# Two blocks of a small model: two linear-attention heads' values and the queries are projected between the second and third forgetting-attention pair, the fourth pair last but for the gates

## The chip, the cores and the metric

The kernel runs on one core of one Trainium2 chip. The metric is the device time of one launch in microseconds. The kernel before was timed three times: median 2360.22 us, lowest 2359.61, highest 2360.74.

## The reference, cut to what matters

A sequence of 528 rows (16 learned rows and 512 of the input, 1024 wide) passes through two layers of a first block and one layer of a second one. The change touches only the mixer of the first block, which each of its two layers runs once:

```python
xn = rms_norm(h, attn_norm[i])
gq, gk, gv, gr, glr, fq, fk, fv, ff = jnp.split(xn @ w_in[i], cuts, axis=-1)
# gated linear attention, 4 heads: per chunk of 64 rows a state S = decay*S + k^T v; out = q @ S
o_gla = rms_norm(gla_chunk_causal(gq/8, gk, gv, log_a), gla_norm) * silu(gr)
# forgetting attention, 8 heads of 64: softmax(q k^T / 8 + c_t - c_s) v, causal
o_fox = rms_norm(forgetting_attention(fq, fk, fv, log_f), fox_norm)
h = h + concatenate([o_gla, o_fox]) @ w_out[i]
```

## The kernel before, in words

**Jobs.** The work is a list of projection jobs. A job multiplies 128 columns of a weight by the whole sequence, 528 rows as two halves of 264. Float32 accuracy is had by splitting weight and activation into a rounded high part and a rest, so each of the 8 k-steps has three passes of two matmuls and a job has 48 matmuls (`steps`, line 304, matmul on line 322). A job accumulates into one of two PSUM buffers (`psm`, line 49). When its matmuls are done, its evacuation copies the result out, scaled by the row's norm (`scaled`, line 374: VectorE on line 378 or 380); the buffer is then free for the job after the next. Weights come by DMA on SP's queue, 256 columns (two jobs) a load, and are split on ScalarE and VectorE (lines 273 and 274) two jobs ahead.

**Steps behind the jobs.** An evacuation also pushes small functions into a queue: transposes, attention units, norms. While a later job issues its matmuls, `steps` takes functions from the queue at a rate of 1.3 for each k-step and issues their instructions between the matmuls (`pump`, line 299). So functions ride along with later jobs, and what is pushed late rides late.

**The mixer's jobs**, after a small one for the gates of decay. Names: fk, fq, fv with p = 0 to 3 are keys, queries and values of a pair of forgetting-attention heads; gk0 and gk1 are the keys of two linear-attention heads each, gq0 and gq1 the queries; gv0 to gv3 and gr0 to gr3 the values and output gates of one head. The order before is

```
gk0 gk1 fk0 fq0 fv0 | fk1 fq1 fv1 gv0 gv1 | fk2 fq2 fv2 gv2 gv3 | fk3 fq3 fv3 gq0 gq1 | gr0 gr1 gr2 gr3
```

and then the eight jobs of the output projection, `out0` to `out7`, whose k-steps read `mix[0..3]` (linear-attention heads) and `mix[4..7]` (forgetting pairs) in the order 4, 5, 6, 7, 0, 1, 2, 3.

**A forgetting pair** (`fox_pair`, line 630) is ten units, for each of two heads and five row blocks: scores with softmax (Exp on ScalarE, line 575), transposes of the weights (line 600), values (line 620). A unit's stages are pushed one behind the other, so that units overlap in a pipe. Then follow `fox_norm` (line 647: transposes on line 654, VectorE 655, ScalarE 659, VectorE 661 and 186, a power on GpSimd 187), `fox_scale` (line 668) and `fox_tail` (line 672: transposes 681, ScalarE 682, VectorE 182), which writes `mix[4 + p]`. For pairs 0 to 2 these ride in the pipe. For pair 3 the pipe is emptied at once into the queue, `fox_scale` is pushed by gq0's evacuation and `fox_tail` by gq1's.

**Linear attention.** gv3's evacuation pushes the states (line 740, a chain on VectorE), each gq's the outputs and their norms (`gla_out`, lines 794 to 801 and 754). The scaling by the norm (line 762) is pushed by gq1 for heads 0 and 1 and by gr0 for heads 2 and 3. A gr's evacuation applies Silu on ScalarE (line 915). `gla_tail` (line 816: transposes 824 and 828, VectorE 829, ScalarE 830, VectorE 179) makes `mix[h]`; for h = 0 and 1 it is queued, for h = 2 and 3 it is issued inside `out0`, ahead of the k-step of index 2 and 4.

**Order.** Each engine runs its own list strictly in order. The framework makes these lists when the kernel is built, from what is ready by its own costs and from priorities. Evacuations get a raised priority; instructions wrapped in `pin` (lines 668, 681, 762, 824, 828) stay behind the instruction issued before them on their engine. Nothing moves at run time.

Of the kernel before, what the change touches and what calls it, by code (L numbers as in the profile page):

```python
# [36 lines left out]
class Net:  # L37
# [592 lines left out]
    def fox_pair(self, st, i, p, mix, last):  # L630
        self.push(lambda: self.fox_prep(st, p), lambda: self.fox_gates(st, p))
        for b in range(2):
            self.push_unit(self.fox_unit(st, b, 0, None))
        for hf in range(2):
            for b in range(2):
                group = {}
                for j in (2 * hf + 1, 2 * hf + 2):
                    stages = self.fox_unit(st, b, j, group)
                    if hf == 1 and b == 1 and j == 4:
                        stages += [lambda: self.fox_norm(st)]  # L640
                        if not last:
                            stages += [None, lambda: self.fox_scale(st), lambda: self.fox_tail(st, i, p, mix)]
                    self.push_unit(stages)
        if last:
            self.drain_pipe()
# [193 lines left out]
    def layer(self, i):  # L839
        nc, a = self.nc, self.a  # L840
        w_in = a["w_in"][i]
        st = dict(e=[], dec=[], kt=[], gvt=[], S={}, S0={}, om={}, on={}, gr={}, gk={}, gq={}, gv={}, scale={})
        fst = [dict() for _ in range(4)]
        mix = [None] * 8
# [27 lines left out]
        def ev_fk(p):  # L872
            return lambda ps: self.fox_k(fst[p], self.scaled(ps, FULL, self.rs))

        def ev_fq(p):
            def f(ps):
                t = self.scaled(ps, FULL, self.rs, extra=0.125)
                fst[p]["q"] = [self.stack_q(t, b) for b in range(2)]
            return f

        def ev_fv(p):
            def f(ps):
                fst[p]["fv"] = self.scaled(ps, FULL, self.rs)
                self.fox_pair(fst[p], i, p, mix, p == 3)
            return f

        def ev_gk(m):
            def f(ps):
                t = self.scaled(ps, FULL, self.rs)
                self.push(lambda: self.gla_k(st, m, t))  # L890
            return f
# [10 lines left out]
        def ev_gq(m):  # L902
            def f(ps):
                self.gla_q(st, m, self.scaled(ps, FULL, self.rs, extra=0.125))
                self.push(*self.gla_out(st, m))
                if m == 0:
                    self.push(lambda: self.fox_scale(fst[3]))
                else:
                    self.push(*st["scale"][0], lambda: self.fox_tail(fst[3], i, 3, mix))
            return f  # L910

        def ev_gr(h):
            def f(ps):
                t = self.scaled(ps, FULL, self.rs)
                nc.scalar.activation(t, t, AF.Silu)
                tail = lambda: self.gla_tail(st, i, h, t, mix)
                if h == 0:
                    self.push(tail, *st["scale"][1])
                elif h == 1:
                    self.push(tail)  # L920
                else:
                    first_out["at"] = {**first_out.get("at", {}), 2 * h - 2: [tail]}
            return f

        rest = [(256, ev_gk(0)), (384, ev_gk(1))]
        rest += [(512 + 128 * h, ev_gv(h)) for h in range(4)]
        rest += [(0, ev_gq(0)), (128, ev_gq(1))]
        pieces = []
        for p in range(4):
            fox = [(2064 + 128 * p, ev_fk(p)), (1552 + 128 * p, ev_fq(p)), (2576 + 128 * p, ev_fv(p))]  # L930
            r = rest[2 * p:2 * p + 2]
            pieces += r + fox if p == 0 else fox + r
        pieces += [(1024 + 128 * h, ev_gr(h)) for h in range(4)]
        for x in range(0, len(pieces), 2):
            (c0, e0), (c1, e1) = pieces[x:x + 2]
# [11 lines left out]
        def ev_out(k):  # L947
            def f(ps):
                h = self.h[k]
                nc.vector.tensor_tensor(self.v(h, TO), self.psv(ps, TO), self.v(h, TO), op=ALU.add)  # L950
                if k == 0:
                    nxt["hs"] = []
                    nxt["acc"] = self.G()
                    if t0:
                        nc.gpsimd.memset(nxt["acc"][:, :t0], 1.0)
                nxt["hs"].append(self.hs_of(h[:, t0:], self.vec("ffn", 8 * i + k), None, t0, L))
                self.sq_acc(nxt["acc"], h[:, t0:], k == 0, 1.0, t0, L)
            return f
# [4 lines left out]
        for k in range(KT):  # L963
            if k % 2 == 0:
                ch = self.chunk([(self.wcols(w_out, 128 * k, 256), 0)], KT)
            self.job(ch, 128 * (k % 2), lambda: mix, TO, ev_out(k))
            if k == 0:
                first_out = self.jobs[-1]
            self.jobs[-1]["order"] = [4, 5, 6, 7, 0, 1, 2, 3]
            self.jobs[-1]["flush"] = k == 0  # L970


# [699 lines left out]
```

## Time and profile before

| | us |
|---|---|
| median of 3 runs | 2360.22 |
| the profiled execution | 2361.31 |
| its span | 2359.5 |
| TensorE (PE) busy | 2318.5 |
| VectorE (DVE) busy | 1378.4 |
| ScalarE (ACT) busy | 952.2 |
| GpSimd (POOL) busy | 248.3 |

The span is the time from the first to the last instruction; the profiled execution adds 1.8 us around it. The mixer of the first layer lies at about 40 to 262 us of the span, that of the second at about 720 to 942 us. An engine's busy time is an average over stages with different limits. PE's idle time is 41 us in all, and the question for this kernel is where it lies.

### The profile page before, as it was taken

Reading aid. Unit: us, or ns where it says so; the run is one execution under the profiler, and the core shown is the slowest. Engines: PE = TensorE matmul, PEld = TensorE weight load, DVE = VectorE, ACT = ScalarE, POOL = GpSimd, SP = SyncE. Lnnn points to the kernel's source line nnn. Section 1 sums busy time; section 2 is a strip of 40 time slices with the busy share of each in tenths; the row PEclk is TensorE's granted clock in tenths of the full one; section 3 lists DMA queues with packets and bytes.
Section 4 is the critical chain, followed back from the end, with each engine's and each line's share of the span. In section 5 each row is a group of like instructions: output and inputs, shape, how many; then the busy total and the mean of one; then the engine's idle time right before and its main releaser. Section 6 shows DMA issues by size and latency. Waiting matters only on the chain.

```text
span 2359.5 us, 37628 instructions
## 1 busy us (share of the span) xinstructions
PE 2318.5 (98%) x15703; PEld 2133.4 (90%) x15703; DVE 1378.4 (58%) x2480; ACT 952.2 (40%) x1641; POOL 248.3 (11%) x261
## 2 busy tenths in 40 slices
PE   7999999999999999999999999999999999999998
PEld 6999999999998998999998889988999888888888
DVE  6667556465556677466464666797454454333335
ACT  6555434233346655343242544322233533222225
POOL 3111210000021112200000121100000002101012
PEclk9999999999999999999999999999999999999999
DMA  4211122222231211222223222222212222232323
GB/s 115 73 55 55 55 90 90 90 90 89 96 87 54 55 55 54 90 90 90 90 84 105 85 76 88 90 90 90 89 55 72 72 90 90 92 105 89 98 85 130
DMA packets 217072, 196.77 MB, mean 83 GB/s; under 512 B 8987, under 2 KB 214791, under 8 KB 216903
## 3 DMA queue, kind: packets, MB, share of 16 engines
q1 hardware_dynamic: 216903, 194.37, 25.9%
q8 instruction: 124, 2.03, 0.3%
q14 instruction: 45, 0.37, 0.1%
HBM read 192.26 MB, written 2.10 MB: 82 GB/s over the span
## 4 chain that ended last, share of the span: by engine, by line
PE 66%; ACT 1%; DVE 1%; issue 1%; POOL 0%; DMA 0%; POOLq 0%; ACTq 0%; SPq 0%
PE mm L322 59%; PE valuesT L1158 1%; PE scoresS L1141 1%; PE foxV L620 1%; PE attend_pT L480 1%; PE foxT L600 0%; ACT wh L273 0%; PE foxS L510 0%; POOL g L204 0%; PE spreadS L223 0%; PE foxS L511 0%; PE idx L510 0%; DMA raw<-in_w_down_dram 0%; PE to_tokensT L463 0%; PE idx L511 0%
## 5 line engine op out<-in xcount | busy, mean ns | idle before, releaser
L322 PE MATMUL mm<-g,wh 128*128 128x264 f32 (+3 forms) x9168 | 1883.0, 316 | 13.8 <-DVE g L378 11.7
L322 PEld LDWEIGHTS mm<-g,wh 128*128 128x128 f32 x9168 | 1393.3, 190 | 113.8 <-issue 12.8
L322 PE MATMUL mm<-g,wl 128*128 128x264 f32 (+3 forms) x4552 | 1161.0, 313 | 0.0
L322 PEld LDWEIGHTS mm<-g,wl 128*128 128x128 f32 x4552 | 752.2, 189 | 50.4
L273 ACT ACTIVATE wh<-raw 128x1024 fp32r<-128x1024 f32 (+1 forms) x369 | 384.9, 1043 | 947.9 <-PE mm L322 808.8
L274 DVE TENSOR_TENSOR wl<-raw,wh 128x1024 fp32r<-128x1024 f32 (+1 forms) x369 | 445.1, 1206 | 66.0 <-ACT wh L273 55.8
L378 DVE TENSOR_TENSOR g<-mm,g 128x528 f32<-128x528 f32 (+2 forms) x228 | 158.5, 696 | 318.7 <-PE mm L322 315.4
L204 POOL TENSOR_TENSOR g<-g,g 128x528 f32<-128x528 f32 (+3 forms) x49 | 71.4, 1469 | 914.9 <-ACT g L203 568.0
L179 DVE TENSOR_TENSOR g<-g,g 128x512 fp32r<-128x512 f32 (+3 forms) x131 | 92.1, 703 | 38.2 <-ACT g L1010 29.0
L1035 DVE TENSOR_TENSOR g<-mm,g 128x528 f32<-128x528 f32 (+1 forms) x48 | 33.6, 700 | 119.3 <-PE mm L322 119.3
L992 ACT ACTIVATE g<-g,cv 128x528 f32<-128x528 f32 (+1 forms) x88 | 72.1, 819 | 17.8 <-DVE g L378 17.7
L1421 POOL TENSOR_TENSOR g<-g,g 128x512 f32<-128x512 f32 x22 | 38.9, 1766 | 283.9 <-ACT g L1420 283.9
L995 DVE SCALAR_TENSOR_TENSOR g<-g,cv,g 128x526 f32<-128x526 f32 (+1 forms) x88 | 66.9, 760 | 3.1
L994 DVE SCALAR_TENSOR_TENSOR g<-g,cv,g 128x527 f32<-128x527 f32 (+1 forms) x88 | 66.3, 754 | 1.8 <-ACT g L992 1.8
L179 DVE TENSOR_TENSOR g<-foxT,g 128x128 fp32r<-128x128 f32 (+1 forms) x160 | 50.5, 340 | 20.3 <-ACT g L605 18.0
L1006 ACT ACTIVATE g<-g 128x528 f32<-128x528 f32 (+1 forms) x44 | 28.1, 639 | 84.0 <-DVE g L995 84.0
L1008 DVE TENSOR_TENSOR g<-g,g 128x528 f32<-128x528 f32 (+1 forms) x44 | 30.8, 701 | 32.4 <-ACT g L1006 32.4
L575 ACT ACTIVATE g<-g,sm 128x144 f32<-128x144 f32 (+2 forms) x80 | 43.1, 538 | 16.0 <-DVE sm L571 15.3
L187 POOL TENSOR_TENSOR sm<-sm,mhalf 128x10 f32<-128x10 f32 (+3 forms) x29 | 37.2, 1290 | 115.2 <-DVE sm L186 114.9
L605 ACT ACTIVATE g<-foxT 128x256 fp32r<-128x256 f32 (+1 forms) x96 | 33.1, 345 | 27.6 <-PE foxT L600 22.5
L1010 ACT ACTIVATE g<-g 128x528 fp32r<-128x528 f32 (+1 forms) x44 | 28.1, 638 | 33.1 <-DVE g L1008 33.1
L1452 DVE TENSOR_TENSOR g<-mm,g 128x512 f32<-128x512 f32 x16 | 11.1, 692 | 49.9 <-PE mm L322 49.9
(282 smaller groups left out, 1706.8 us busy)
## 6 DMA issues: line engine op xcount, KB each, us to landing
raw<-in_w_up_dram SPq DMA_DIRECT2D x50, 1024.0 KB
raw<-in_w_in_dram SPq DMA_DIRECT2D x44, 1024.0 KB
raw<-in_w_down_dram SPq DMA_DIRECT2D x28, 896.0 KB
raw<-in_w_in_dram SPq DMA_DIRECT2D x28, 512.0 KB
raw<-in_w_out_dram SPq DMA_DIRECT2D x12, 1024.0 KB
raw<-in_w_down_dram SPq DMA_DIRECT2D x12, 1024.0 KB
raw<-in_w_gate_dram SPq DMA_DIRECT2D x10, 1024.0 KB
raw<-in_w_up_dram SPq DMA_DIRECT2D x10, 512.0 KB
```

Source lines behind the costliest of these rows:

```text
L179: (eng or self.nc.vector).tensor_tensor(out, x, hi.bitcast(F32), op=ALU.subtract)
L187: self.nc.gpsimd.tensor_tensor(out, v[:rows, :n], self.mhalf[:rows, :n], op=ALU.pow)
L204: nc.gpsimd.tensor_tensor(acc[:, t0:t1], tmp[:, t0:t1], acc[:, t0:t1], op=ALU.add)
L273: keep(nc.scalar.activation(hi[:, :K], src, AF.Copy))
L274: keep(nc.vector.tensor_tensor(lo[:, :K], src, hi[:, :K].bitcast(F32), op=ALU.subtract))
L322: nc.tensor.matmul(ps[:, b, :n], lhsT=w[:, k, :], rhs=x[:, t:t + n], start=(ki == 0 and pi == 0), stop=(ki == len(order) - 1 and pi == len ...
L378: self.nc.vector.tensor_tensor(self.v(out, toks), self.psv(ps, toks), self.v(rs, toks), op=ALU.mult)
L575: nc.scalar.activation(P[:qs, :N], P[:qs, :N], AF.Exp, scale=-1.0, bias=m, accum_out=col)
L992: nc.scalar.activation(A[:, lo:], U[:, lo:], AF.Identity, bias=self.vec("cb", 44 * i + t), scale=cw(2))
L994: nc.vector.scalar_tensor_tensor(A[:, s1:], U[:, s1 - 1:L - 1], cw(1), A[:, s1:], op0=ALU.mult, op1=ALU.add)
L995: nc.vector.scalar_tensor_tensor(A[:, s0:], U[:, s0 - 2:L - 2], cw(0), A[:, s0:], op0=ALU.mult, op1=ALU.add)
L1421: nc.gpsimd.tensor_tensor(z[:, META:], z[:, META:], self.rs[:, META:], op=ALU.mult)
```

## The change

Only the order of the mixer's jobs and of what rides along with them changes; no instruction of the computation is added or removed. The new order of the jobs is

```
gk0 gk1 fk0 fq0 fv0 | gv0 fk1 fq1 fv1 gv1 | gv2 gv3 gq0 gq1 fk2 fq2 fv2 | fk3 fq3 fv3 | gr0 gr1 gr2 gr3
```

Pair 3's `fox_scale` and `fox_tail` ride in its pipe as those of the other pairs do. All scaling of linear attention is pushed by gq1. The tails of heads 2 and 3 move to index 0 and 2 of `out0`, and all output jobs read `mix` in the order 4, 5, 6, 0, 1, 2, 3, 7. The loads per layer stay five of two adjacent column blocks and seven pairs of loads of one block each.

```diff
@@ fox_pair
                     if hf == 1 and b == 1 and j == 4:
                         stages += [lambda: self.fox_norm(st)]
-                        if not last:
-                            stages += [None, lambda: self.fox_scale(st), lambda: self.fox_tail(st, i, p, mix)]
+                        stages += [None, lambda: self.fox_scale(st), lambda: self.fox_tail(st, i, p, mix)]
                     self.push_unit(stages)
@@ layer, ev_gq
                 self.push(*self.gla_out(st, m))
-                if m == 0:
-                    self.push(lambda: self.fox_scale(fst[3]))
-                else:
-                    self.push(*st["scale"][0], lambda: self.fox_tail(fst[3], i, 3, mix))
+                if m == 1:
+                    self.push(*st["scale"][0], *st["scale"][1])
@@ layer, ev_gr
-                if h == 0:
-                    self.push(tail, *st["scale"][1])
-                elif h == 1:
+                if h < 2:
                     self.push(tail)
                 else:
-                    first_out["at"] = {**first_out.get("at", {}), 2 * h - 2: [tail]}
+                    first_out["at"] = {**first_out.get("at", {}), 2 * h - 4: [tail]}
@@ layer
-            r = rest[2 * p:2 * p + 2]
-            pieces += r + fox if p == 0 else fox + r
+            pieces += {0: rest[:2] + fox, 1: rest[2:3] + fox + rest[3:4], 2: rest[4:] + fox, 3: fox}[p]
@@ layer, output jobs
-            self.jobs[-1]["order"] = [4, 5, 6, 7, 0, 1, 2, 3]
+            self.jobs[-1]["order"] = [4, 5, 6, 0, 1, 2, 3, 7]
```

## Rows read from the trace of the kernel before

**Rows 1.** The page: busy time by engine, and the chain of waits.

```profile
PE 2318.5 (98%) x15703; PEld 2133.4 (90%) x15703; DVE 1378.4 (58%) x2480; ACT 952.2 (40%) x1641; POOL 248.3 (11%) x261
...
PE 66%; ACT 1%; DVE 1%; issue 1%; POOL 0%; DMA 0%; POOLq 0%; ACTq 0%; SPq 0%
```

**Rows 2.** PE's waits, whole span: us in total, times, longest.

```profile
PE mm L322 <- DVE g L378: 11.7, 3, 4.8
```

**Rows 3.** PE's first matmuls of `out0`, both layers: start, us, instruction, idle before.

```profile
258.67 1.22 PE L322 MATMUL mm<-g,wh 128*128 128x264 f32 x4 [3.49 <-DVE g L378]
...
938.99 0.72 PE L322 MATMUL mm<-g,wh 128*128 128x258 f32 x4 [3.49 <-DVE g L378]
```

**Rows 4.** VectorE at the end of the projections, first layer (same columns).

```profile
252.88 1.29 DVE L762 TENSOR_TENSOR g<-g,sm 128x512 f32<-128x512 f32 x2
...
254.42 0.89 DVE L829 SCALAR_TENSOR_TENSOR g<-gla_tailT,cv,g 128x272 f32<-128x272 f32 x2
256.06 1.22 DVE L274 TENSOR_TENSOR wl<-raw,wh 128x1024 fp32r<-128x1024 f32 x1 [0.75 <-ACT wh L273]
257.21 0.70 DVE L179 TENSOR_TENSOR g<-g,g 128x528 fp32r<-128x528 f32 x1
257.82 1.32 DVE L378 TENSOR_TENSOR g<-mm,g 128x528 f32<-128x528 f32 x2
```

**Rows 5.** Windows of 2 us: engines' busy us, granted PE clock, DMA share, GB/s.

```profile
258.00:260.00 2.00, 1.33 (x6) 1.36 (x7) 1.14 (x2) 1.26 (x2) 0.00 (x0) 0.51 0.00 0
260.00:262.00 2.00, 2.00 (x11) 2.00 (x11) 0.00 (x0) 0.00 (x0) 0.00 (x0) 0.50 0.03 8
...
938.00:940.00 2.00, 1.01 (x8) 1.04 (x9) 1.46 (x3) 1.12 (x2) 0.00 (x0) 1.00 0.00 0
```

**Rows 6.** Evacuations of the output jobs: `out0` to `out2` first layer, `out0` second.

```profile
268.72 0.71 DVE L950 TENSOR_TENSOR g<-mm,g 128x528 f32<-128x528 f32 x1 [0.85 <-PE mm L322]
...
274.55 0.71 DVE L950 TENSOR_TENSOR g<-mm,g 128x528 f32<-128x528 f32 x1 [3.01 <-PE mm L322]
...
280.39 0.71 DVE L950 TENSOR_TENSOR g<-mm,g 128x528 f32<-128x528 f32 x1 [3.03 <-PE mm L322]
...
946.48 0.69 DVE L950 TENSOR_TENSOR g<-mm,g 128x516 f32<-128x516 f32 x1 [0.84 <-PE mm L322]
```

**Rows 7.** Pair 3's norm, first layer, from its transposes to `mix[7]`.

```profile
236.68 0.38 PE L654 MATMUL foxN<-ident,g 128*128 128x128 f32 x2
...
242.97 0.83 DVE L668 TENSOR_TENSOR o<-o,sm 128x640 f32<-128x640 f32 x1
...
245.19 0.93 ACT L682 ACTIVATE g<-foxN,cv 128x272 fp32r<-128x272 f32 x2
...
249.13 0.48 DVE L182 SCALAR_TENSOR_TENSOR g<-foxN,cv,g 128x256 fp32r<-128x256 f32 x1
```

**Rows 8.** ScalarE around the first Silu: the last softmax before it, and its table load.

```profile
228.96 0.73 ACT L575 ACTIVATE g<-g,sm 128x528 f32<-128x528 f32 x1
...
237.13 1.28 ACT L915 ACT_TABLE_LOAD   x1
```

**Rows 9.** Windows in the columns of rows 5: three mixer stretches, one of the second block.

```profile
200.00:220.00 20.00, 19.86 (x158) 18.50 (x158) 14.56 (x45) 12.00 (x38) 5.68 (x9) 1.00 0.16 54
220.00:240.00 20.00, 19.49 (x157) 18.28 (x155) 12.81 (x38) 14.08 (x39) 0.90 (x3) 1.00 0.17 53
240.00:260.00 20.00, 16.51 (x131) 16.28 (x132) 17.43 (x35) 10.66 (x21) 7.89 (x8) 0.95 0.16 54
180.00:200.00 20.00, 19.77 (x161) 19.10 (x160) 17.60 (x43) 6.87 (x13) 1.09 (x2) 1.00 0.17 53
...
1835.00:1845.00 10.00, 10.00 (x55) 8.33 (x54) 5.51 (x15) 7.43 (x12) 0.00 (x0) 1.00 0.25 86
```

**Rows 10.** VectorE by line, 180 to 262 us: busy us, mean ns, idle before.

```profile
L740 DVE SCALAR_TENSOR_TENSOR g<-g,dec,gla_statesS 64x128 f32<-64x128 f32 x28 | 9.1, 347 | 0.7
...
L754 DVE TENSOR_REDUCE sm<-g 128x4 f32<-128x512 f32 (+1 forms) x6 | 3.5, 589 | 0.0
```

## The prediction

> **What bounds the kernel now.** I read the page's busy times first. PE is busy for 2318.5 of 2359.5 us, and the chain of waits that ended last is two thirds PE [rows 1]. No edit here changes PE's instructions, so only PE's 41 us of idle time can move, together with the time it spends at half clock. The waits of PE, longest first, come second: the first row puts 11.7 us in three waits down to a projection matmul that waits for line 378 on VectorE, the evacuation of a job [rows 2]. The timeline of PE places two of the three: they stand right ahead of the first matmul of `out0`, 3.49 us in each layer [rows 3]. The third is at the start of the second layer's mixer and is not touched. So the stage that counts is the end of the projections, and the wait that ends last there is a VectorE one.
>
> VectorE's timeline tells what it did instead [rows 4]. `out0` needs the PSUM buffer of gr2. PE had stopped at 258.67 - 3.49 = 255.18 us, at the end of gr3; gr2 had ended one job and two tails earlier, near 248. Its evacuation runs at 257.82, together with gr3's. Ahead of it in VectorE's list stand the scaling of heads 2 and 3 (line 762), the tails of heads 0 and 1 (lines 829, 179) and a weight split (line 274). VectorE is busy 17.43 of the 20 us from 240 to 260, against 14.56 and 12.81 in the two windows before [rows 9]. It is full there because everything that was pushed late rides there.
>
> After the wait the granted clock is 0.51 and 0.50 in the first layer and 1.00 in the second [rows 5]. What this costs comes from `out0` itself: from PE's restart to its evacuation it takes 268.72 - 258.67 = 10.05 us in the first layer and 946.48 - 938.99 = 7.49 us in the second [rows 3, 6]. The second has 258 columns instead of 264, some 0.13 us of a job of 280.39 - 274.55 = 5.84 us [rows 6]. So the half clock costs 2.4 us.
>
> **The change part by part.** I counted through the code which step rides with which job.
>
> *What leaves the end.* Before, the outputs of linear attention and their norms ride in gr1, the scaling (762) and both tails in gr2. Now the outputs ride in gq1 and fk2 and all the scaling in fk2. What gr1 to gr3 lose on VectorE is six reduces of line 754, 3.5 us [rows 10], and the scaling of four heads, 2 x 1.29 us [rows 4], some 6 us, and the GpSimd powers ahead of them.
>
> *What comes to the end.* Pair 3's units rode in gq0, gq1 and gr0 and ride now in gr0, gr1 and gr2. Its norm, scale and tail were issued in gr1 and gr2 and are now issued in gr3, steps 0 and 2; the tails of heads 0 and 1 go from gr2 to gr3, steps 3 and 4. The decisive point is that no tail is issued any more before gr2's evacuation. In gr2 there are only units, as in gr0 before, and the windows that held units have PE at 19.86 and 19.49 of 20 us [rows 9]. So I expect gr2's evacuation inside gr3's time, and the wait of 3.49 us goes in both layers: 2 x 3.49 = 7.0 us. Bounds: 0 (another order of VectorE's list, below) to 7.0. With it goes the half clock, 2.4 us; bounds 0 (another idle time brings it back) to 2.4.
>
> *What is late next.* `mix[7]`. From the transposes of the norm to its last instruction it took 249.61 - 236.68 = 12.9 us [rows 7]. Of this, 7.1 us go to the end of the scale (243.80), and after ScalarE's part ended at 245.19 + 0.93 = 246.12 VectorE came to the last piece only at 249.13, 3 us later, because of the work that now is gone. Without that the chain is 246.12 + 2 x 0.48 - 236.68 = 10.4 us. It can begin 0.8 us into gr3 (after k-step 0) and in the worst case at the end of gr3's own matmuls, 5.8 us, so `mix[7]` is ready 11.2 to 18.7 us after gr3 began. It is needed in the last k-step of `out0`. The two tails in `out0` cost 7.49 - (5.84 - 0.13) = 1.8 us; gr3 has two tails and nine more transposes, so 5.84 + 1.8 + 1.0 = 8.6 us (the 1.0 an estimate: half a tail); the last k-step begins 7 x 0.73 + 1.8 = 6.9 us later, at 15.5 us. PE waits between 0 and 3.2 us here. I take 1.0 us a layer, nearer to the lower end, as the late start is the rarer one: 2.0 us in both.
>
> *Tails of heads 2 and 3.* They are issued two k-steps earlier and `mix[2]`, `mix[3]` are read one earlier, which leaves one k-step (0.73 us) more between. Nothing to pay, provided gr3's evacuation isn't late; if it is, as gr2's was, the bound is again 3.49 us a layer.
>
> *What comes to the middle.* States, outputs and scaling fall in gq0, gq1 and fk2. VectorE then has there 32 x 0.347 = 11.1 us of states [rows 10], 3.5 + 2.6 of norms, three evacuations of 0.7 and three splits of 1.22, together 23 us, against three jobs of 5.84 us and the small matmuls between them. It is a full stretch. The nearest one is 180 to 200 us, with the states in it: VectorE 17.60, PE 19.77 [rows 9]. I take 0; bounds 0 and 3.49 us a layer. What spills over has fq2 behind it, in which nothing rides. PE's order of transposes can shift by tenths of a microsecond either way; that is 0.
>
> *ScalarE's tables.* Before, the last softmax is at 228.96 us and the first Silu brings a table load of 1.28 us at 237.13, one a layer [rows 8]. Now the Silus of gr0, gr1 and gr2 come among pair 3's softmaxes, so up to five loads, four more: 5.1 us of ScalarE a layer. In the windows of the units ScalarE is busy 12.00 and 14.08 of 20; with the loads some 78%. In the second block, where softmaxes and sigmoids alternate, ScalarE is busy 7.43 of 10 us and PE 10.00 of 10 [rows 9]. I cost them at 0; upper bound 5.1 us a layer. The Trainium skill, in "ScalarE: Activation LUTs", section "Table sets: the hidden batching unit", says to do all calls of one table set before those of another, and this change breaks that rule; its section "What ACT_TABLE_LOAD costs" puts a switch at 2.66 us with a drain, of which our row shows 1.28 and no drain. By that figure it would be an estimated 10.6 us of ScalarE a layer.
>
> *Loads.* Their number and sizes stay, and the DMA engines are used at 0.16 to 0.17 in these windows [rows 9]. SP's queue only takes them in another order: 0.
>
> *The sum.* -7.0 - 2.4 + 2.0 = -7.4 us. The profiled execution took 2361.31 us (its span 2359.5 and 1.8 around it), so 2353.9; it lies 1.1 us above the median of the runs shown, so for a median I take 2360.2 - 7.4 = 2352.8, rounded to 2353.
>
> **The rivals.**
>
> *The wait stays.* VectorE's list is made when the kernel is built, and the trace doesn't say why gr2's evacuation was put behind the tails although its priority is raised. If the same order comes again for gr3 or gr2, `out0` or its tails wait as before. For it: the tails of heads 0 and 1 still ride with a gr job, and the same sequence is in both layers. Against it: the four scalings ahead of them are gone. Time: 2360, or about 2356 if one layer gains.
>
> *The wait moves to the middle.* The 23 us of VectorE work make the evacuation of gq0 or gq1 late, and fk2 or fq2 wait for a PSUM buffer: 2 x 3.49 us given back, 2358 to 2360. Against it: 180 to 200 us.
>
> *The last pair ends too late (slower).* This is one chain: table loads stretch pair 3's softmaxes, its units run on into gr3, and its norm begins and ends late, with only one job behind it where three were before. At worst 18.7 + 5.1 = 23.8 us against 15.5: PE waits 8.3 us in `out0`, and with the half clock behind it 10.7 us a layer. That is 21.4 - 9.4 = 12 us slower, 2372. It decides from 9.4 / 2 = 4.7 us a layer on, that is a wait of 2.3 us with the half clock behind it. For it: PE waits in its order and there is no other job to fill in. Against it: PE at 10.00 of 10 where tables alternate [rows 9]. The Trainium skill's rule on table sets would have it so.
>
> **How the numbers follow.** The forecast (2351 to 2355.5, likeliest 2353) gets 0.50; the wait that stays 0.22; the wait in the middle 0.08; the slower case 0.20, most of it between 2362 and 2368. No change that can be told is within 0.2%, or 4.7 us, here 2355.5 to 2364.9. Faster: 0.50 and 0.03 of the one-layer case. Slower: 0.19. The low end is the sum without the 2.0 us, 2350.8, less 1 us for small waits of PE in the windows of the units (20 - 19.49 and 20 - 19.86, in two layers [rows 9]), so 2349.5. The high end reaches into the slower case, 2365.5.
>
> **What would show it.** In the changed kernel, the wait of `out0`'s first matmul for line 378 is gone from both layers; VectorE's list has gr2's evacuation ahead of lines 829; the window behind has clock 1.00; there are three to five table loads among pair 3's softmaxes and no PE wait in their stretch; a wait, if any, stands ahead of `out0`'s last k-step, for line 182, and is under 2.3 us. It is wrong if a wait for line 378 is still there or stands in gq1 to fq2, or if line 182 (or 179) holds PE for over 2.3 us.

## The result and the profile after

The changed kernel takes 2383.99 us (median of 4 runs, 2382.68 to 2385.43), the kernel before 2359.91 in the same comparison. The ratio is 1.0101, 95% interval 1.0090 to 1.0113: 24.1 us slower. I had forecast 7 us faster. The profiled execution has a span of 2382.3 us, 22.8 more than before.

In the changed kernel the line numbers have shifted: `fox_norm` is on lines 646 to 661, `fox_scale` on 667, the tail's transposes on 680, linear attention's tail on 823 to 829, Silu on 912, the evacuation of an output job on 944. Up to line 638 nothing has moved.

From the page, the busy times, which answer to [rows 1]:

```profile
PE 2332.7 (98%) x15703; PEld 2142.3 (90%) x15703; DVE 1379.0 (58%) x2480; ACT 965.0 (41%) x1649; POOL 250.2 (11%) x261
```

PE issues the same 15703 instructions and is busy 14.2 us longer; the same matmuls run slower, in part at half clock (below). ScalarE has eight instructions more, the table loads: 8 x 1.28 = 10.2 of the 12.8 us by which it is busier. VectorE is as busy as before.

PE's waits of the whole span, longest first (us in total, times, longest), against [rows 2]:

```profile
PE foxN L680 <- DVE o L667: 7.3, 2, 3.6
PE mm L322 <- DVE g L378: 4.8, 1, 4.8
PE foxV L620 <- DVE g L179: 4.7, 4, 1.7
```

The wait of `out0` for line 378 is gone from the list in both layers; the one left stands at the start of the second layer's mixer, as before. By this view alone the forecast would look right. In its place stand the tail of pair 3, which waits for its scaling, and pair 3's units, which wait for their weights' low parts (179).

What filled the wait is seen on PE's timeline of the first layer (start, us, instruction, idle before), which answers to [rows 3]:

```profile
247.09 0.41 PE L322 MATMUL mm<-g,wl 128*128 128x264 f32 x2
...
252.84 0.80 PE L620 MATMUL foxV<-g,fvms 128*128 128x256 f32 x2 [1.68 <-DVE g L179]
...
258.02 1.91 PE L620 MATMUL foxV<-g,g 128*128 128x256 f32 x8
...
260.01 1.23 PE L322 MATMUL mm<-g,wh 128*128 128x264 f32 x4
...
263.34 0.41 PE L322 MATMUL mm<-g,wl 128*128 128x264 f32 x2
267.36 1.30 PE L680 MATMUL foxN<-ident,o 128*128 128x128 f32 x5 [3.61 <-DVE o L667]
269.35 0.47 PE L823 MATMUL gla_tailT<-ident,om 128*128 128x128 f32 x1 [0.69 <-DVE g L182]
...
270.84 0.47 PE L823 MATMUL gla_tailT<-ident,om 128*128 128x128 f32 x1 [0.17 <-DVE g L828]
...
271.99 1.55 PE L322 MATMUL mm<-g,wh 128*128 128x264 f32 x4
```

gr3's matmuls end at 247.50; before, they ended at 255.18. PE is 7.7 us early there, because the gates' matmuls have run ahead of pair 3's units. From 247.50 to 260.01 it has only the units, each stage of which waits for another engine: 12.5 us. It is not all idle: from 248 to 260 us PE is busy 8.6 of the 12 us, from 252 on at half clock. Then come 18 matmuls, the three k-steps of `out0` that read `mix[4]` to `mix[6]`. From 263.75 to 271.99 there is no projection again, 8.2 us: the norm, scale and tail of pair 3, then two tails of linear attention. Five k-steps of `out0` are still to come, but the next two read `mix[0]` and `mix[1]`, and the tails that make these (269.35 and 270.84) stand behind pair 3's tail in PE's list. So none of the five runs beside the norm. The second layer has the same two gaps.

VectorE's timeline of the same stretch, for [rows 4]:

```profile
256.64 1.30 DVE L179 TENSOR_TENSOR g<-foxT,g 128x256 fp32r<-128x256 f32 x3 [0.44 <-ACT g L605]
257.86 0.70 DVE L378 TENSOR_TENSOR g<-mm,g 128x528 f32<-128x528 f32 x1
260.44 0.42 DVE L624 TENSOR_TENSOR g<-foxV,g 64x256 f32<-64x256 f32 x1 [1.88 <-ACT g L622]
261.70 0.69 DVE L654 TENSOR_TENSOR o<-foxN,sm 128x512 f32<-128x512 f32 x1 [0.84 <-PE foxN L653]
...
266.38 0.83 DVE L667 TENSOR_TENSOR o<-o,sm 128x640 f32<-128x640 f32 x1 [2.07 <-POOL sm L187]
```

The evacuation of gr2 runs at 257.86. Before, it ran at 257.82. It is as late as it was; only what stands ahead of it is another thing, the units' line 179 instead of the tails. Since PE itself was held by a unit until then, no wait for line 378 shows. The chain of the norm after it, 261.70 to 267.21, is a wait of one engine for the next. The evacuation of `out0`, line 944, comes at 282.09, where it came at 268.72 [rows 6].

Windows of 2 us in the columns of [rows 5]:

```profile
250.00:252.00 2.00, 0.80 (x4) 0.45 (x4) 2.00 (x7) 1.31 (x5) 0.00 (x0) 1.00 0.78 275
252.00:254.00 2.00, 1.17 (x5) 1.17 (x6) 1.18 (x5) 0.49 (x3) 0.00 (x0) 0.53 0.00 0
254.00:256.00 2.00, 2.00 (x11) 1.79 (x9) 0.21 (x1) 0.38 (x1) 0.00 (x0) 0.50 0.00 0
...
264.00:266.00 2.00, 0.00 (x0) 0.00 (x0) 0.28 (x2) 0.00 (x0) 1.81 (x2) 0.95 0.00 0
266.00:268.00 2.00, 0.65 (x3) 0.68 (x4) 0.83 (x1) 0.00 (x0) 0.35 (x1) 0.50 0.00 0
...
274.00:276.00 2.00, 2.00 (x11) 2.00 (x11) 1.81 (x4) 0.61 (x2) 0.00 (x0) 0.50 0.00 0
276.00:278.00 2.00, 2.00 (x18) 2.00 (x18) 1.29 (x3) 0.84 (x2) 0.00 (x0) 0.99 0.00 0
```

The granted clock falls to half (1.2 of 2.4 GHz) at 252 us, inside the first stretch, comes back at 262 and falls again at 266, inside the second: some 20 us at half clock in this layer. For [rows 9], the windows of 20 us (same columns), with the clock at 1.00 in those before them:

```profile
240.00:260.00 20.00, 16.60 (x104) 14.79 (x104) 10.76 (x31) 11.89 (x28) 0.00 (x0) 0.80 0.16 53
260.00:280.00 20.00, 15.54 (x87) 14.09 (x86) 10.68 (x20) 7.17 (x11) 2.16 (x2) 0.68 0.00 1
```

In the kernel before, PE had 131 matmuls from 240 to 260 us; here it has 104, and 87 in the next 20 us, with VectorE at 10.8 and 10.7 us instead of 17.4. No engine is full there.

ScalarE, for [rows 8]: the table loads among pair 3's softmaxes and the last softmax.

```profile
225.75 1.28 ACT L912 ACT_TABLE_LOAD   x1
...
231.08 1.28 ACT L575 ACT_TABLE_LOAD   x1
...
240.30 1.28 ACT L912 ACT_TABLE_LOAD   x1
...
242.43 1.28 ACT L575 ACT_TABLE_LOAD   x1
...
251.23 0.73 ACT L575 ACTIVATE g<-g,sm 128x528 f32<-128x528 f32 x1
...
260.43 1.28 ACT L912 ACT_TABLE_LOAD   x1
```

Five loads, as counted in the prediction. The last softmax comes at 251.23; before, it was at 228.96.

The place of the loss can be fixed by PE's progress: the time from the mixer's first projection matmul to its n-th one, changed kernel less kernel before, worked out from the traces. (That first matmul is at 13.96 and 700.26 us in the kernel before; the 40 and 720 us given above as the mixer's start are too late.) At the end of the matmuls up to gr3 it is -7.6 us in the first layer and -4.0 in the second; 48 matmuls later (one job) it is +10.4 and +16.5, and there it stays to the end of `out7`. So 18.0 and 20.5 us are lost within one job's worth of PE's list, at `out0`. Of these, 7.6 and 6.5 us had been gained just before, because the units' matmuls had been left behind the gates'; the net loss is 10.4 and 14.0 us. (The figures of the second layer, -4.0 and +16.5, hold another 2.5 us that it loses in its first job. Kernels with and without the edits have 0 to 2.7 there, so I don't put it down to the change.)

### The profile page after: what moved, and what is told of

Same layout as the page of the kernel before. It is cut to its first block, busy times and chain, and to the rows that moved or that the text cites. A ratio compares the mean times of both kernels' runs of the same rounds, so it can differ in the third digit from the quotient of the medians.

```text
span 2382.3 us, 37657 instructions
## 1 busy us (share of the span) xinstructions
PE 2332.7 (98%) x15703; PEld 2142.3 (90%) x15703; DVE 1379.0 (58%) x2480; ACT 965.0 (41%) x1649; POOL 250.2 (11%) x261
## 4 chain that ended last, share of the span: by engine, by line
PE 65%; ACT 1%; DVE 1%; issue 1%; POOL 1%; DMA 0%; POOLq 0%; ACTq 0%; SPq 0%; DVEq 0%
PE mm L322 59%; PE valuesT L1152 1%; PE foxV L620 1%; PE scoresS L1135 1%; PE attend_pT L480 1%; DMA raw<-in_w_down_dram 0%; PE foxT L600 0%; ACT wh L273 0%; PE foxS L510 0%; POOL g L204 0%; PE spreadS L223 0%; PE foxS L511 0%; POOL sm L187 0%; PE idx L510 0%; PE to_tokensT L463 0%
```

## The experiments

The theories. **Cover:** behind the last pair's values only four jobs are left; pair 3's units and norm form a chain of waits, and PE runs out of projections to put beside it. **Tables:** the Silus of the gates among the softmaxes stretch that chain. **Rate:** the units are only issued too late beside the gates. **Pipe and tails:** the places of scale, tail and reading order cost by themselves. "Progress" below is the figure just defined, at the end of gr3's matmuls and then two jobs later, first layer / second layer.

### e1: no Silu

The gates are copied instead of put through Silu (left out: the gate function).

```diff
-                nc.scalar.activation(t, t, AF.Silu)
+                nc.scalar.activation(t, t, AF.Copy)
```

> The changed kernel with the Silu of the output gates replaced by a copy of the same size (the gate function is left out), so ScalarE needs no table load between pair 3's softmaxes (before the edit: 5 loads a layer from gr0 to gr3, 1.28 us each). Theory 1, too little cover: pair 3's chain of units, norm and tail ends about 12 us after gr3's matmuls whatever the tables do, since only four jobs stand behind fv3; the loads account for at most 3 us of it a layer: 2377 to 2384 us. Theory 2, tables: the loads are what makes the softmaxes late, 5 to 12 us a layer: 2360 to 2374 us, with the softmaxes of pair 3 ending before gr3's matmuls do.

2375.07 us (ratio 1.0064, 1.0049 to 1.0079): 8.9 us less than the change, between the two ranges. Progress -2.7 / -1.3, then +4.3 / +8.6. Eight table loads are gone from the kernel (20 instead of 28) and with them 4.5 us a layer; 15 us of the loss stay without them. Pair 3's last softmax now ends at 248.6 us, before gr3's matmuls (252.7), as theory 2 had it. PE's list is another as well: the units stand among the gates' matmuls, and the stretch without a projection ahead of `out0` is 2.85 us instead of 12.5. That of the norm stays, at 8.3 us.

### e2: queries behind the last pair's values again

```diff
-            pieces += {0: rest[:2] + fox, 1: rest[2:3] + fox + rest[3:4], 2: rest[4:] + fox, 3: fox}[p]
+            pieces += {0: rest[:2] + fox, 1: rest[2:3] + fox + rest[3:4], 2: rest[4:6] + fox, 3: fox + rest[6:]}[p]
```

> The changed kernel with the two query jobs gq0 and gq1 put back behind fv3; everything else stays as changed (values early, scale and tail in pair 3's pipe, tails in out0 at 0 and 2, reading order with 7 last). Six jobs instead of four stand behind fv3. Theory 1, cover: the loss is gone, 2352 to 2362 us, and PE has no stretch without projection matmuls at the end. If instead the tails in the pipe or the reading order with 7 last cost the time (theory 3): 2375 us or more.

2369.44 us (1.0045, 1.0030 to 1.0060): 14.6 us less than the change, still 9.7 over before, and in neither range. Progress +3.3 / +5.1, then +0.4 / +6.4. With the outputs of linear attention at the end again, waits for line 378 are back (9.4 us, 5 times). The edit moves the tables too: one load a layer is left instead of five. So the 14.6 us are cover and tables together, and what two jobs more are worth by themselves this run doesn't tell.

### e3: a higher rate beside the gates

```diff
+            if x == 20:
+                self.jobs[-2]["rate"] = 2.0
...
+                first_out["rate"] = 1.3
```

> The changed kernel with the rate at which queued functions are taken raised from 1.3 to 2.0 a k-step during gr0 to gr3, and back to 1.3 from out0. Pair 3's units are then all issued by the middle of gr2 instead of its end. Theory 4, issued too late: the chain ends some 6 us earlier a layer, 2370 to 2374 us. Theory 1, cover with a chain bound by latency: the place in PE's list follows readiness, not issue, and the time moves little: 2379 to 2386 us.

2391.98 us (1.0135, 1.0119 to 1.0150), slower by 8 us than the change, outside both ranges and in spite of three table loads a layer instead of five: the rate theory falls. The units now stand ahead of the gates' matmuls in PE's list, and PE waits inside the gates' jobs: the longest stretch without a projection matmul, from 239.88 to 255.19 us, lies before gr3's end. More steps a k-step don't shorten a chain whose length is that of its waits.

### e4: the old order of jobs, the other edits kept

```diff
-            pieces += {0: rest[:2] + fox, 1: rest[2:3] + fox + rest[3:4], 2: rest[4:] + fox, 3: fox}[p]
+            r = rest[2 * p:2 * p + 2]
+            pieces += r + fox if p == 0 else fox + r
```

> The changed kernel with the job order of before; only the other edits stay (scale and tail of pair 3 in its pipe, all scaling of linear attention pushed by gq1, tails in out0 at 0 and 2, reading order with 7 last). Theory 1, cover: six jobs behind fv3, no loss, 2350 to 2363 us. Theory 3, tails and reading order cost the time: 2372 us or more. My forecast's wait for line 378 ahead of out0 (3.5 us a layer) should still be there if the scaling ahead of the tails makes it: 2358 to 2363; gone if the order of the tails does: 2350 to 2356.

2364.14 us (1.0016, 1.0007 to 1.0026), 1.1 us above the range of the cover theory. The order of jobs costs 19.9 of the 24.1 us; the other edits 4.4. With the old order one table load a layer is left, so the 19.9 us hold the tables as well as the cover. The wait of `out0` for line 378 is still there, at 1.9 us a layer.

### e5: Silu written with the tail

```diff
-                nc.scalar.activation(t, t, AF.Silu)
-                tail = lambda: self.gla_tail(st, i, h, t, mix)
+                def tail():
+                    nc.scalar.activation(t, t, AF.Silu)
+                    self.gla_tail(st, i, h, t, mix)
```

> The changed kernel, the whole computation, but each Silu of a gate is issued with the tail of its head and not with the gate's evacuation, so that it comes after the last pair's softmaxes. If the switches between Exp and Silu cost what the kernel without Silu showed (8.9 us in both layers), the time is 2374 to 2378 us and one or two table loads a layer are left. If that gain came from the Silu instructions themselves and not from the switches, or if the late Silu with its load of 1.28 us now holds the tails (four tails in two layers, up to 2 us each), it is 2381 to 2388. By the cover theory 15 us stay over the kernel before in either case.

2380.06 us (1.0080, 1.0065 to 1.0095), between the two expectations, because the edit did not do what it was for: the loads are still five, and stand where they stood (first layer).

```profile
227.18 1.28 ACT L913 ACT_TABLE_LOAD   x1
...
232.52 1.28 ACT L575 ACT_TABLE_LOAD   x1
...
242.86 1.28 ACT L913 ACT_TABLE_LOAD   x1
```

The list for ScalarE is made from what is ready, and the gate is ready long before its tail. So the run says nothing on tables. The units' stretch ahead of `out0` is 9.1 and 8.7 us instead of 12.5; why that gains 3.9 us I did not follow.

### e9: Silu tied behind the last softmax

The whole computation; a bias of zero made from the softmaxes' sums makes the Silu wait for them. Against e5, cut to what matters:

```diff
+                    if "z" not in nxt:
+                        nxt["z"] = self.S()
+                        nc.vector.tensor_scalar(nxt["z"][:, :8], fst[3]["sums"][:, 2:10], 0.0, None, op0=ALU.mult)
-                    nc.scalar.activation(t, t, AF.Silu)
+                    nc.scalar.activation(t, t, AF.Silu, bias=nxt["z"][:, :1])
```

> The changed kernel, the whole computation, with each Silu in the tail of its head and with a bias of zero made from the sums of the last pair's softmaxes, so that it cannot run before them (one small VectorE instruction more a layer). In the kernel before this one the Silus were only written later, and the list for ScalarE put them among the softmaxes again: the five table loads stayed. If the switches cost the 8.9 us that the kernel without Silu showed, one load a layer is left near the end and the time is 2374 to 2379 us. If a Silu of 1.3 us with its load on the path of the first tail costs as much as it saves, it is 2380 to 2386.

2375.61 us (1.0066, 1.0051 to 1.0081), 8.4 us less than the change. In the first layer's stretch one load is left, behind the softmaxes (ScalarE), and the tail's wait stands as it was (PE's waits):

```profile
257.52 1.28 ACT L916 ACT_TABLE_LOAD   x1
```

```profile
PE foxN L680 <- DVE o L667: 7.9, 2, 4.0
```

With the gate computed in full this is the same gain as without it (8.9): it goes with the switches, 1.05 us for each of the eight loads that go. The Trainium skill, in "ScalarE: Activation LUTs", section "Table sets: the hidden batching unit", says to finish all calls of one set before those of another; here this was worth 8.4 us. Its section "What ACT_TABLE_LOAD costs" has 2.66 us a switch, of which the load is 1.28 and the rest a drain; the rows here have 1.28 us a load, and the time moved by less than that.

The gain is not the loads' time alone. PE's list changed with them, as in e1 (first layer, the last of gr3's matmuls and the first of `out0`):

```profile
251.78 0.41 PE L322 MATMUL mm<-g,wl 128*128 128x264 f32 x2
...
255.04 0.75 PE L322 MATMUL mm<-g,wh 128*128 128x264 f32 x4 [1.11 <-DVE g L378]
```

The stretch of the units is 2.85 us instead of 12.5, and gr3 ends 4.7 us later, because the units stand among the gates' matmuls again. So the table loads among the softmaxes go with the list that put the units behind gr3. No run here tells which part of the 8.4 us is the loads and which the list.

### e8: five jobs behind the last pair's values

```diff
-            pieces += {0: rest[:2] + fox, 1: rest[2:3] + fox + rest[3:4], 2: rest[4:] + fox, 3: fox}[p]
+            pieces += {0: rest[:2] + fox, 1: rest[2:3] + fox + rest[3:4], 2: rest[4:7] + fox, 3: fox + rest[7:]}[p]
```

> The changed kernel with its second query job moved back behind the last pair's values, so that five jobs stand behind them: between the change with four (2384.0) and the kernel with both query jobs moved back, with six (2369.4). If what counts is how much matmul work is left beside the last pair's chain, a job (5.8 us) more takes about half of the 14.6 us away: 2375 to 2379. If it is a threshold (six jobs cover, five do not), 2381 to 2386; if five cover as well as six, 2367 to 2372.

2381.12 us (1.0092, 1.0075 to 1.0108): by its median the threshold case, one job hardly helps; the interval, 2377.9 to 2385.7 us, reaches into the range of half the gain. Progress +3.7 / +6.3 at gr3's end, then +6.5 / +11.9. The clock is at 0.83 in one window of 10 us and at 1.00 in those around it, so the gap at the end is smaller; but a stretch of 7.8 us with the units alone now stands ahead of gr3, the outputs of the second query job now meet the units, and `out0` waits for the buffer again (PE, first layer):

```profile
262.27 0.91 PE L322 MATMUL mm<-g,wh 128*128 128x264 f32 x4 [3.06 <-DVE g L378]
```

So "a job more, 7 us less" is not borne out. I read it so that what rides with the added job takes most of its cover away; that was not varied. Three table loads a layer are left instead of five, and by e9's 1.05 us a load these four would be an estimated 4.2 us, more than the 2.9 that the run gained.

### e10: the chain's end inside out0

On the change: all tails in `out0`'s k-steps 0 to 3, pair 3's scale in k-step 1, its tail in k-step 5.

```diff
-                        stages += [None, lambda: self.fox_scale(st), lambda: self.fox_tail(st, i, p, mix)]
+                        if not last:
+                            stages += [None, lambda: self.fox_scale(st), lambda: self.fox_tail(st, i, p, mix)]
...
-                if h < 2:
-                    self.push(tail)
-                else:
-                    first_out["at"] = {**first_out.get("at", {}), 2 * h - 4: [tail]}
+                at = first_out.setdefault("at", {})
+                at[h] = [tail]
+                if h == 3:
+                    at[1] = at[1] + [lambda: self.fox_scale(fst[3])]
+                    at[5] = [lambda: self.fox_tail(fst[3], i, 3, mix)]
```

> The changed kernel with the end of its order loosened: all four tails of linear attention are issued in out0's k-steps 0 to 3, and the last pair's scale in k-step 1 and its tail in k-step 5, so that out0's first six k-steps (4.4 us) and four tails are beside its norm chain, which stood alone for 8.5 us in each layer. If that stall is lack of cover, 5 to 7.5 us a layer go, and some half clock: 2364 to 2374. If the chain's own length sets the end and out0 can't start earlier, the stall only moves to out0's last k-steps: 2380 to 2386. The stretch of the units (12.8 us in each layer) stays in either case, so the kernel before is not reached.

2368.17 us (1.0038, 1.0025 to 1.0051): 15.8 us less than the change. The gap of the norm is gone: PE has no wait for the scaling any more. The stretch of the units is left, 10.2 and 12.5 us. The edit does two things at once: it takes pair 3's scale and tail out of the pipe, and it puts the heads' tails ahead of that tail in PE's list, so that `out0`'s other k-steps run beside the norm. No run here tells what each gains with the new job order. Windows of 10 us, first the changed kernel, then this one, in the columns of [rows 5]:

```profile
250.00:260.00 10.00, 7.20 (x31) 6.16 (x32) 5.35 (x16) 3.23 (x10) 0.00 (x0) 0.61 0.16 55
260.00:270.00 10.00, 5.70 (x30) 5.12 (x29) 3.91 (x7) 3.95 (x6) 2.16 (x2) 0.67 0.01 2
270.00:280.00 10.00, 9.83 (x59) 8.97 (x58) 6.77 (x13) 3.22 (x5) 0.00 (x0) 0.70 0.00 0
```

```profile
250.00:260.00 10.00, 6.18 (x44) 5.16 (x44) 7.33 (x20) 5.32 (x16) 0.00 (x0) 1.00 0.23 82
260.00:270.00 10.00, 9.97 (x81) 9.55 (x79) 7.66 (x15) 4.25 (x8) 2.16 (x2) 1.00 0.01 2
...
930.00:940.00 10.00, 7.29 (x40) 5.90 (x39) 6.01 (x20) 5.19 (x14) 0.00 (x0) 0.75 0.32 107
940.00:950.00 10.00, 9.31 (x60) 8.99 (x60) 6.66 (x14) 5.10 (x9) 0.96 (x1) 0.74 0.00 0
```

In the first layer the clock stays at 1.00 in spite of the units' waits, and progress ends at -0.9 there; in the second it falls, and progress ends at +7.7. From gr3's end that is a loss of 6.4 us in the first and 11.8 in the second. The two layers run the same order, so the 5.4 us between them are about what the half clock adds to a gap. In the changed kernel it is at most (0.39 + 0.33 + 0.30) x 10 = 10.2 us in the first layer, from the first three rows; how much of that PE would have waited anyway these rows don't tell.

### e11: both edits

e9 and e10 together.

```diff
+                    nc.scalar.activation(t, t, AF.Silu, bias=nxt["z"][:, :1])
...
+                    at[5] = [lambda: self.fox_tail(fst[3], i, 3, mix)]
```

> The two edits before this one together (Silus tied behind the last softmaxes; the end of the last pair inside out0). If tables and cover add up, it gains what both gain alone: 2357 to 2368 us. If the late Silus lengthen the tails that are now out0's cover, it gains less than the second edit alone: 2368 to 2376. The 12.8 us stretch with only units is left, shorter by the four table loads (5.1 us).

2362.61 us (1.0010, 1.0000 to 1.0020): 21.4 of the 24.1 us are back, against 8.4 + 15.8 = 24.2 for the two alone, and the kernel is 2.9 us over before. The stretch of the units did not stay, as I had expected: it is 2.85 us in both layers, as in e9. With the job order of the change untouched, the tables (with the list that goes with them) and the uncovered norm chain with its half clock are nearly the whole loss; the clock is 1.00 in all its windows from 240 to 290 and from 930 to 980 us.

### e6: the kernel before, all tails inside out0

It tests how I had read the wait in the kernel before.

```diff
-                if h == 0:
-                    self.push(tail, *st["scale"][1])
-                elif h == 1:
-                    self.push(tail)
-                else:
-                    first_out["at"] = {**first_out.get("at", {}), 2 * h - 2: [tail]}
+                if h == 0:
+                    self.push(*st["scale"][1])
+                first_out["at"] = {**first_out.get("at", {}), h: [tail]}
```

> The kernel before, with one edit: the tails of heads 0 and 1 are issued inside out0 too (k-steps 0 and 1, with heads 2 and 3 at 2 and 3), and no longer with gr2. It tests how I read the wait of 3.49 us in the kernel before: gr2's evacuation stands in VectorE's list behind the tails that are issued in the same job. If that is so, the wait goes in both layers and the half clock behind it in the first: 2359.7 - 7.0 - 2.4 = 2350.3, so 2349 to 2354. If the list has it behind the scaling or behind the weight split for another reason, the wait stays: 2358 to 2362. If the later tails make mix[0] and mix[1] late, PE waits in the middle of out0 instead: 2360 to 2366.

2350.02 us (0.9956, 0.9942 to 0.9971): 10.2 us faster than before, 34 faster than the change, and the lowest median of this study. VectorE of the first layer, for [rows 4]:

```profile
249.22 0.70 DVE L378 TENSOR_TENSOR g<-mm,g 128x528 f32<-128x528 f32 x1
...
254.27 0.71 DVE L378 TENSOR_TENSOR g<-mm,g 128x528 f32<-128x528 f32 x1 [1.22 <-PE mm L322]
254.90 0.49 DVE L829 SCALAR_TENSOR_TENSOR g<-gla_tailT,cv,g 128x272 f32<-128x272 f32 x1
```

gr2's evacuation is at 249.22 instead of 257.82, gr3's waits for its matmuls alone, and the tails come behind both. `out0` starts without a wait.

### e7, e12, e14: pair 3's scale and tail in its pipe

Three kernels with the job order of before. e7 has the pipe edit and all scaling at once, e12 only the scaling at once, e14 is e7 with empty stages between.

```diff
 e7, against the change
-            pieces += {0: rest[:2] + fox, 1: rest[2:3] + fox + rest[3:4], 2: rest[4:] + fox, 3: fox}[p]
+            r = rest[2 * p:2 * p + 2]
+            pieces += r + fox if p == 0 else fox + r
-                    first_out["at"] = {**first_out.get("at", {}), 2 * h - 4: [tail]}
+                    first_out["at"] = {**first_out.get("at", {}), 2 * h - 2: [tail]}
-            self.jobs[-1]["order"] = [4, 5, 6, 0, 1, 2, 3, 7]
+            self.jobs[-1]["order"] = [4, 5, 6, 7, 0, 1, 2, 3]
```

> The kernel before with two edits of the change alone: the scale and the tail of the fourth pair ride as stages of its last unit, and all scaling of linear attention is issued at once behind its second query job; jobs, tails and reading order as before. The kernel with the job order of before and all other edits took 2364.1. If these two edits make its 4.4 us, the time is 2363 to 2366. If the tails' places in out0 and the reading order make them, it is 2358.5 to 2361.5.

2365.60 us (1.0022, 1.0013 to 1.0032), in the first range: the two edits together make the 4.4 us.

```diff
 e12, against the kernel before
-                    self.push(*st["scale"][0], lambda: self.fox_tail(fst[3], i, 3, mix))
+                    self.push(*st["scale"][0], lambda: self.fox_tail(fst[3], i, 3, mix), *st["scale"][1])
-                if h == 0:
-                    self.push(tail, *st["scale"][1])
-                elif h == 1:
+                if h < 2:
```

> The kernel before with one edit: the scaling of all four heads of linear attention is pushed behind its second query job and not half of it behind gr0. With the pipe edit beside it the kernel took 2365.6. If the pipe edit makes the 5.4 us (the tail's transposes wait 1.7 us a layer for the scale right ahead of them), this one takes 2358.5 to 2361.5. If the scaling at once makes them, 2363.5 to 2366.5.

2352.97 us (0.9968, 0.9956 to 0.9980): faster than before, which neither case had. The wait of `out0` in the first layer, first in e7, then here:

```profile
260.26 0.75 PE L322 MATMUL mm<-g,wh 128*128 128x264 f32 x4 [3.57 <-DVE g L378]
```

```profile
255.18 0.73 PE L322 MATMUL mm<-g,wh 128*128 128x264 f32 x4 [1.53 <-DVE g L378]
```

So the scaling at once takes 2 us of the 3.49 us before, and the clock stays at 1.00 behind what is left of that wait: 2 x 2 for the wait in both layers and 2.4 for the half clock in the first are 6.4 of the 6.8 us gained. The pipe edit, which I had not priced at all, costs 2365.6 - 2353.0 = 12.6 us beside it.

```diff
 e14, against e7
-                        stages += [None, lambda: self.fox_scale(st), lambda: self.fox_tail(st, i, p, mix)]
+                        late = 4 if last else 0
+                        stages += [None] * (1 + late) + [lambda: self.fox_scale(st)] + [None] * late
+                        stages += [lambda: self.fox_tail(st, i, p, mix)]
```

> The kernel with the order of jobs, tails and reading of before, all scaling at once, and the last pair's scale and tail as stages of its last unit (2365.6 us), with four empty stages more ahead of the scale and four ahead of the tail. Without those stages in the pipe the kernel took 2353.0. If their 12.6 us come from the tight spacing (the tail's transposes wait 1.65 us a layer for the scale, PE's order is held there, and the outputs' norms on VectorE come later), 2352 to 2357. If they come from the place ahead of linear attention's outputs in the queue, however far apart they are, 2362 to 2368.

2356.43 us (0.9983, 0.9974 to 0.9993): 9.2 of the 12.6 us go with nothing but distance. But not as I had put it, by PE's wait for the scale (line 669 in e14), which is longer here than in e7. PE's waits of e14:

```profile
PE mm L322 <- DVE g L378: 4.8, 1, 4.8
PE foxN L682 <- DVE o L669: 4.5, 2, 2.3
```

In e7 the second of these took 3.3 us and the first 11.9 in three waits. What the close tail costs is seen at line 378: in e7 gr2's evacuation runs at 259.51, here at 251.88. I read it so that the pinned tail pushes the outputs' norms back in VectorE's list and the evacuation behind them; that order was not varied by itself.

### e13: e6 and e12 together

```diff
-                    self.push(*st["scale"][0], lambda: self.fox_tail(fst[3], i, 3, mix))
+                    self.push(*st["scale"][0], lambda: self.fox_tail(fst[3], i, 3, mix), *st["scale"][1])
-                if h == 0:
-                    self.push(tail, *st["scale"][1])
-                elif h == 1:
-                    self.push(tail)
-                else:
-                    first_out["at"] = {**first_out.get("at", {}), 2 * h - 2: [tail]}
+                first_out["at"] = {**first_out.get("at", {}), h: [tail]}
```

> The kernel before with the two edits that made it faster alone, together: all four tails of linear attention issued in out0's k-steps 0 to 3 (alone 2350.0 us, the wait for line 378 gone) and all scaling pushed behind the second query job (alone 2353.0 us, that wait at 1.5 us in the first layer). If both work on the one wait of out0, they do not add up: 2348 to 2351. If they take different time away, 2342 to 2346. If the scaling now crowds gr0 or gr1, 2352 to 2358.

2353.17 us (0.9965, 0.9953 to 0.9977). That lies in the range given to crowding, but the interval overlaps that of e6, so it can't be told from e6 alone. The two don't add up. Both work on the one wait of `out0`, and with the tails gone there is nothing left of it for the scaling to take.

## Why the prediction was wrong

*What bounds the kernel now:* right. The wait for line 378 was worth what the sum gave it: 7.0 + 2.4 = 9.4 us, and e6, in whose trace it is gone, gains 10.2.

*What comes to the end:* this step failed. "In gr2 there are only units, as in gr0 before, and the windows that held units have PE at 19.86 and 19.49 of 20 us. So I expect gr2's evacuation inside gr3's time." It ran at 257.86, 10.4 us after gr3's matmuls had ended. Two things were wrong in it. The windows show units beside projections; they don't say how long the units take when the projections have run out, and behind gr0 stood three jobs' matmuls, behind gr2 stands one. And I looked for tails ahead of the evacuation in VectorE's list, where units stand in the way as well: their line 179 waits for ScalarE, which waits for PE.

*What is late next:* the mechanism was named, its size was not. I took one chain, `mix[7]`, at 1.0 us a layer with 8.6 us of gr3 beside it. This step failed as well, and its term in the sum, 1.0 us, is the one that was furthest off. The sum let `out0` run up to its last k-step beside the chain. In fact pair 3's units end 12 us after gr3's matmuls, so gr3 was no cover, and PE stopped after three k-steps of `out0`, not ahead of the last: it waited 3.6 us for the scaling (line 667) and not for line 182, with the heads' tails and five k-steps behind that wait in its list. The stretches are 8.2 us for the chain and 12.5 us for the units ahead of it, with the half clock in both. On PE's progress the net loss is 10.4 and 14.0 us a layer. (The bound of 18.7 us is 5.8 + 12.9; with the chain of 10.4 us that the text itself takes, it is 16.2.)

*ScalarE's tables:* the count of five loads a layer was right and the cost of 0 was not; e1 and e9 have 4.2 to 4.5 us a layer, near the upper bound of 5.1. The price comes with a change of PE's list that I had not thought of: with the loads the units stand behind gr3, without them among the gates (12.5 and 2.85 us). The row of the second block where tables alternate at a full PE was the wrong neighbour; I take it that PE has other work to do there, while here the softmaxes are on the path.

*What comes to the middle:* right. No wait for line 378 stands in gq1 to fq2, and the window 180 to 200 us has PE at 19.95 of 20.

*Tails of heads 2 and 3, and the pipe:* the reading order and the tails' places are not what costs (with the old job order; e4 and e7, with and without them, take 2364.1 and 2365.6). The pipe edit had no term of its own in the sum; with the old job order it costs 12.6 us beside e12.

*The rivals:* "The last pair ends too late" came true with the chain, the table loads and the half clock as described. Its worst case, 2372, was 12 us short, because it let the units run on into gr3 and not past its end. Its argument against itself, PE at 10.00 of 10 where tables alternate, is the row that misled.

## What to carry to other kernels

Before work is moved ahead of a chain of waits, count what is left beside it to the next point where everything must be done: a chain's price is its length without cover, not its busy time. A wait that leaves the list of waits hasn't gone if the instruction it waited for still ends at the same time; look at when that one runs. A run that moves jobs can move other things with them (e2 and e4 took the table loads away too): count these before the gain is put down to one cause. And where one engine's list is in order, take the late producers out of the way (e6) before you move the consumers.

## What was not expected of the hardware

The clock did not answer to the length of a gap alone. In the changed kernel it fell behind a window in which PE was busy 0.80 of 2 us, and stayed at 0.50 through windows with PE at 2.00 of 2. In e10 the first layer held 1.00 through 10 us in which PE was busy 6.18, with the same waits of the units, while the second fell to 0.75. A forecast of such a gap has to carry both cases; between the two layers of e10 they differ by some 5.4 us.

A Silu that was only written later in the program still ran where it had run (e5): the framework makes the list by readiness, and there it took a data dependency to move it (e9).
